# Where a turned activation tile is put together, and when the last one of a unit is joined

## The chip, the cores and the metric

The kernel runs on one core of one Trainium2 chip. The metric is device time in microseconds (us), the median of three runs of the kernel before: 1449.74 us (1449.1 to 1450.11). Engines are named as the profile names them: PE is TensorE, PEld its weight loads, DVE is VectorE, ACT is ScalarE, POOL is GpSimd, SP is the engine whose queue issues most DMAs.

## What is computed

One decoder layer for 256 tokens of width 2048: a mixer (a state-space group and an attention group side by side), and then the squared-ReLU MLP, which the change touches:

```
def squared_relu_mlp(u, w_up, w_down):
    hdn = jax.nn.relu(jnp.einsum('bsd,df->bsf', u, w_up))
    return jnp.einsum('bsf,fd->bsd', hdn * hdn, w_down)

h = h + rmsnorm(ff, norm_mlp_post)      # ff = the MLP of rmsnorm(h, norm_mlp_pre)
```

`w_up` is 2048 x 8192, `w_down` 8192 x 2048, all in float32.

## The kernel before, in words

**Products.** Every float32 operand is split in two parts, `hi` and `lo` (lines 148 and 149: ACT copies `hi`, DVE subtracts it to get `lo`), and a product takes three matmuls: hi by hi, hi by lo, lo by hi. Weights come in blocks of 128 x 2 x 512 by DMA from SP's queue into places called `raw` (four of them, and others that are free for a while, such as `ha` and `uc`), are split into one of five pairs of `hi` and `lo` tiles, and are streamed through PE.

**Units.** A unit (function `unit`) makes two column blocks of 512 for both halves of the tokens (t = 0 and 1), in four PSUM banks `acc`; four further banks `more` take partial sums. It goes through the rows of the weight two blocks of 128 at a time; such a step is called a pair here (index k). Some pairs are done in full (`row_tiles`, lines 368 to 370, 24 matmuls); the others by Strassen's scheme with seven products in place of eight (`seven`, lines 455 to 457, 21 matmuls), which needs sums of weights (tiles `e` and one temporary, line 263) and sums of activations (`sums_of_acts`, lines 414 to 417, made once and kept). After the last seven, `combine_new` (lines 464 to 468) reads the banks `more` and writes four tiles in `room["shared"]`: two in `hb`, two in `wpost`. Its last addition, line 468, reads the last of these banks and writes the fourth tile. After that the unit does its last pair, and the next unit takes over with `acc` and `more` exchanged, so that its first products go to the banks that `combine_new` has read.

**The MLP.** The 8192 hidden columns are made in two halves. Each half has four units of the up projection (in the first half the first of these is made in another way), and then two units of the down projection. I number them up 0 to up 3 and down 0, down 1 in each half; up 0 of the first half is the one made in another way. A unit of the up projection has seven pairs in its order, the sevens at places 1, 3, 4 and 6, and an eighth pair at the end.

**Turned tiles.** At the end of an up unit (`up_end`, line 1491) each of the four shared tiles (two blocks, two halves of tokens) is completed, and a generator `turned` is put into the deque `beside` for it. Its first part (lines 1500 to 1503) applies ReLU and square on ACT, copies the 16-bit halves of the words apart into one of two places (`room["halves"]`, in turn; line 1502), and lets SP issue a DMA transpose that writes back into the shared tile (line 1503). Its second part (lines 1505 to 1508) puts the words together again on ACT (line 1506) into a tile called `junk`, and splits that into the `hi` and `lo` of the activations of the down projection (`sh`, `sl`, or `ah`, `al`). A tile is joined, in the words of the title, when this second part is done.

`unit` starts one first part (`pump_beside`) at each place from 2 on, and does a second part (`land_beside`) when two further places have passed. So the tiles of one up unit are handled within the next unit: the first parts at places 2, 3, 4 and 5, the second parts at 4, 5, 6 and, for the fourth tile, later. After the last seven, `drain_beside` finishes all that is left, ahead of `combine_new`. In an up unit that means that the fourth tile is finished at place 6, too; in a down unit all four have been finished by place 7.

**The order.** Most instructions are ordered by a scheduler under priorities; the splits of weights are issued in a line by `issue_after`. What each engine gets is a fixed queue. Temporaries come from `tmp()`, a ring of four tiles named `r`, used by `sums_of_acts`, `seven` and `combine_new`.

Of the kernel before, what the change touches and what calls it, by code (L numbers as in the profile page):

```python
# [10 lines left out]
F32 = mybir.dt.float32  # L11
# [6 lines left out]
P = 128  # L18
# [21 lines left out]
NB = 512  # L40
# [38 lines left out]
def hymba_layer(ctx: ExitStack, tc: tile.TileContext, x, norm_mix_pre, w_in, conv_w, conv_b, dt_bias, a_log,  # L79
# [34 lines left out]
    def part(k):  # L114
        if k < NK:
            return sh, sl, k
        i, r = divmod(k - NK, NK // 2)
        return (*att[i], r)
# [49 lines left out]
    def tmp():  # L168
        if "own" in room:
            room["own"].rotate(1)  # L170
            return room["own"][0]
        return hp.tile([P, NB], F32, name="r", bufs=4)
# [6 lines left out]
    room = {}  # L179
# [13 lines left out]
    def beside_up(raws, turn, halves=None):  # L193

        room["sums"] = [v[:, k:k + KB] for k in range(0, NK // 2, KB) for v in att[1]]
        b = hp.tile([P, NT, NB], F32, name="hb")
        room["shared"] = [[b[:, t] for t in range(NT)],
                          [hp.tile([P, NB], F32, name="wpost", bufs=2) for _ in range(NT)]]
        a = hp.tile([P, 3 * KB, NB], F32, name="ha")
        in_a = [a[:, k:k + KB] for k in range(0, 3 * KB, KB)]  # L200
        halves = in_a.pop(0) if halves is None else halves
        room["halves"] = deque(halves[:, i].bitcast(U16) for i in range(KB))
        room["raw"], room["turn"], room["acts"], room["chain"] = [*raws, *in_a], turn, act_u, True
        room["of_halves"], room["of_a"] = halves, in_a
        sums_of.clear()

    def beside_down():

        a = hp.tile([P, 3 * KB, 2, S], F32R, name="ha")
        room["sums"] = [a[:, k] for k in range(3 * KB)]  # L210
        room["raw"], room["turn"], room["acts"], room["then"] = [mws[2]], 0, part, more_beside_down
        sums_of.clear()
# [60 lines left out]
    def blocks_of(n):  # L273
        return n if isinstance(n, tuple) else (n * NB, (n + 1) * NB)
# [57 lines left out]
    def drain():  # L332
        while waiting:
            pump()
# [3 lines left out]
    def pump_beside():  # L338

        if not beside:  # L340
            return
        work = beside.popleft()
        with tc.issue_after(newest["act"].ins):
            next(work)
        flying.append([work, 0])

    def land_beside(steps=2):

        for one in flying:
            one[1] += 1  # L350
        if flying and flying[0][1] > steps:
            with tc.issue_after(newest["act"].ins):
                next(flying.popleft()[0], None)
        if not (beside or flying) and "then" in room:
            room.pop("then")()

    def drain_beside():
        while beside or flying:
            pump_beside()
            land_beside(0)  # L360
# [11 lines left out]
    def row_tiles(src, c0, ks, acc, acts, first=True, last=True, lag=0, at_end=None, pumps=1, fetch=fetch, halves=None):  # L372


        held = {}
        n = len(ks)
        for i in range(n + lag):
            if i < n:
                held[i] = weights(src, ks[i] * KB, c0, fetch)
            for t, at in ((0, i), (1, i - lag)):  # L380
                if not 0 <= at < n:
                    continue
                if t and halves and at == n - 1:
                    row_tile(acc[t], t, held[at], ks[at], acts, False, last, slice(0, NB // 2))
                    halves(acc[t])
                    acc[t] = bank()
                    row_tile(acc[t], t, held[at], ks[at], acts, True, last, slice(NB // 2, NB))
                else:
                    row_tile(acc[t], t, held[at], ks[at], acts, first and at == 0, last and at == n - 1)
                if at == n - 1 and at_end:  # L390
                    at_end(t, acc[t])
            pump(pumps)
# [12 lines left out]
    def sums_of_acts(k):  # L405

        if k in sums_of:
            return sums_of[k]
        places = room["sums"][2 * len(sums_of):][:2]
        h_, l_, r = room["acts"](k * KB)  # L410
        with tc.high_priority(offset=AHEAD):
            a, c = (tmp().rearrange("p (i s) -> p i s", s=P) for _ in range(2))
            ah_, al_ = (v[:, r:r + KB].bitcast(F32).rearrange("p j (t s) -> p j t s", t=NT) for v in (h_, l_))
            nc.vector.tensor_tensor(a.rearrange("p (j t) s -> p j t s", t=NT), ah_, al_, op=ALU.add)
            nc.vector.tensor_tensor(c[:, 0:2], a[:, 0::3], a[:, 1:2].to_broadcast([P, 2, P]), op=ALU.subtract)
            nc.vector.tensor_tensor(c[:, 2], a[:, 0], c[:, 1], op=ALU.add)
            nc.vector.tensor_tensor(c[:, 3], a[:, 2], c[:, 2], op=ALU.subtract)
            ch, cl = (v.rearrange("p b (t s) -> p (b t) s", t=NT) for v in places)
            split(ch, cl, c)
        sums_of[k] = ch, cl  # L420
        return ch, cl
# [66 lines left out]
    def unit(src, n, order, last, acc, more, combine, lag=0, at_end=(None, None), first=True, ending=None,  # L488
             ready=None, halves=None):


        cols = blocks_of(n)
        sevens = [k for k, by_seven in order if by_seven]
        for i, (k, by_seven) in enumerate(order):
            if i >= 2:
                pump_beside()
            if i + 1 < len(order) and order[i + 1][1]:
                sums_of_acts(order[i + 1][0])
            if by_seven:
                if k == sevens[0]:  # L500
                    drain()
                    if ready:
                        ready()
                seven(src, *cols, k, acc, more, k == sevens[0], k == sevens[-1])
            else:
                for b in range(2):
                    row_tiles(src, cols[b], [k], acc[b::2], room["acts"], first and i == 0, False,
                              fetch=fetch_next)
            land_beside()
            if k == sevens[-1]:  # L510
                drain_beside()
                combine(more)
        for b in range(2):
            if b and ending:
                ended.append(ending(cols[b], last, acc))
            else:
                row_tiles(src, cols[b], last, acc[b::2], room["acts"], False, True, lag if b else 0, at_end[b],
                          fetch=fetch_last if b else fetch_next, halves=halves if b else None)
# [808 lines left out]
    hp = ctx.enter_context(tc.tile_pool(name="hp", bufs=1, reuse_waits="tile"))  # L1327
# [167 lines left out]
    def turned(t, k, r):  # L1495
        room["halves"].rotate(1)
        halves = room["halves"][0]
        ts = slice(t * P, (t + 1) * P)
        words = r.bitcast(U16)
        nc.scalar.activation(r, r, AF.Relu, scale=rmlp[:, t:t + 1])  # L1500
        nc.scalar.activation(r, r, AF.Square)
        nc.scalar.activation(halves.rearrange("p (h n) -> p h n", h=2), words.rearrange("p (n h) -> p h n", h=2), AF.Copy)
        nc.sync.dma_start_transpose(words.rearrange("p (n s) -> p n s", s=P), halves)
        yield
        whole = hp.tile([P, NB], F32, name="junk")
        nc.scalar.activation(whole.bitcast(U16).rearrange("p (n h) -> p h n", h=2), words.rearrange("p (h n) -> p h n", h=2), AF.Copy)  # L1506
        d_h, d_l, i = part(k)
        split(d_h[:, i:i + 4, ts], d_l[:, i:i + 4, ts], whole.rearrange("p (f s) -> p f s", f=4))
# [17 lines left out]
    for hf in range(2):  # L1526
        if hf:
            beside_up([], 0)
        for fb in range(0 if hf else 2, 8, 2):
            unit(w_ups[hf], fb, orders[("up", hf), fb], (7,), acc, more,  # L1530
                 lambda x: combine_new(room["shared"], x), 0, (up_end(fb, 0), up_end(fb + 1, 1)))
            acc, more = more, acc
        if hf == 0:
            beside_down()
            unit(w_down, 0, orders[("down", 0), 0], (14, 15), acc, more,
                 lambda x: combine_new(in_mw(0), x), 0, (onto(0), onto(1)))
            room["raw"], room["turn"] = [new_mw(2)], 0
            room["sums"] += room["sums"][:4]
            unit(w_down, 2, orders[("down", 0), 2], (12, 14, 15), more, acc,
                 onto_new_mw, 0, (onto(2), onto(3)))  # L1540
# [65 lines left out]
```

## Time and profile before

| | |
|---|---|
| median of three runs | 1449.74 us |
| the profiled execution | 1448.34 us |
| its span, first to last instruction | 1446.6 us |
| busy PE, PEld | 1432.3 us (99%), 1201.5 us (83%) |
| busy DVE, ACT, POOL | 1297.6 us (90%), 1000.4 us (69%), 162.6 us (11%) |
| granted TensorE clock | 0.999 |

A row of the timeline has the start in us from the span's start, the duration in us, engine, line, operation, output and inputs, and in brackets how long the engine had been idle and who ended that. The rows called SPq are the issue of DMAs on SP's queue; what they move lands later. The waits are listed as engine, line, whom it waited for, us in total, number of waits, longest. Matmuls overlap: a row says 0.39 us, but the next starts 0.23 us later. The up units of the second half begin at about 1102, 1144, 1185 and 1227 us, and its down 0 at about 1268 us; down 0 of the first half begins at about 939 us.

### The profile page before, as it was taken

To read this page: it belongs to the slowest core of one execution; us is meant where nothing else is said; L and a number is where in the kernel's file an instruction comes from. 1 tells how busy PE (TensorE), PEld (TensorE's weight loads), DVE (VectorE), ACT (ScalarE), POOL (GpSimd) and SP (SyncE) were. 2 spreads that over 40 slices of the span, in tenths; PEclk is the share of its full clock that TensorE was granted. 3 is DMA by queue.
4 is the path that set the end of the run, shared out by engine and by line. 5 is a ranking of instruction groups with operands and counts; after the bars stand their busy time and mean duration, and the time that the engine had idled before them with its cause. 6 is when DMAs were issued, how large, how long until landed. Compare 5 with 4: busy or idle time off the path is not lost. (4 is left out here: it accounts for less than half of the span.)

```text
span 1446.6 us, 20277 instructions
## 1 busy us (share of the span) xinstructions
PE 1432.3 (99%) x6930; PEld 1201.5 (83%) x6930; DVE 1297.6 (90%) x1881; ACT 1000.4 (69%) x1407; POOL 162.6 (11%) x244
## 2 busy tenths in 40 slices
PE   9999999999999999999999999999999999999998
PEld 8888888888888888888888888878888878877886
DVE  7788888988999778689988999999889989989998
ACT  7577669666666666556667668986565689987664
POOL 0201110131111000011100011011111111111000
PEclk9999999999999999999999999999999999999999
DMA  8977656756888648588976799798888999999864
GB/s 268 273 217 225 190 175 186 236 175 195 232 245 255 192 126 251 168 268 261 275 235 213 203 340 288 197 266 244 257 254 262 253 268 288 247 280 293 264 197 150
DMA packets 201927, 340.31 MB, mean 235 GB/s; under 512 B 45616, under 2 KB 48544, under 8 KB 201824
## 3 DMA queue, kind: packets, MB, share of 16 engines
q1 hardware_dynamic: 174304, 279.72, 62.0%
q0 software_dynamic: 19648, 45.63, 15.5%
q10 hardware_dynamic: 7872, 13.68, 2.8%
q8 instruction: 54, 0.88, 0.3%
q14 instruction: 49, 0.40, 0.1%
HBM read 327.39 MB, written 49.84 MB: 261 GB/s over the span
## 5 line engine op out<-in xcount | busy, mean ns | idle before, releaser
L149 DVE TENSOR_TENSOR lo<-raw,hi 128x1024 fp32r<-128x1024 f32 (+1 forms) x390 | 472.6, 1217 | 82.8 <-ACT hi L148 80.6
L148 ACT ACTIVATE hi<-raw 128x1024 fp32r<-128x1024 f32 (+1 forms) x390 | 406.2, 1048 | 170.2 <-PE acc L370 49.1
L526 PE MATMUL acc<-ua,hi 128*128 128x512 f32 x520 | 141.2, 400 | 0.1
L148 ACT ACTIVATE hi<-e 128x1024 fp32r<-128x1024 f32 x66 | 69.7, 1057 | 53.8 <-DVE e L263 50.2
L526 PEld LDWEIGHTS acc<-ua,hi 128*128 128x128 f32 x520 | 91.2, 189 | 14.2 <-ACT hi L148 0.2
L368 PE MATMUL acc<-hi,ua 128*128 128x512 f32 x228 | 90.4, 396 | 0.4 <-DVE wpost L468 0.4
L368 PE MATMUL acc<-hi,sh 128*128 128x512 f32 x220 | 86.6, 394 | 3.0 <-DVE wpost L468 3.0
L369 PE MATMUL acc<-lo,ua 128*128 128x512 f32 x228 | 89.2, 391 | 0.0
L370 PE MATMUL acc<-hi,ua 128*128 128x512 f32 x228 | 89.1, 391 | 0.0
L149 DVE TENSOR_TENSOR lo<-e,hi 128x1024 fp32r<-128x1024 f32 x66 | 80.4, 1218 | 6.4 <-ACT hi L148 6.2
L370 PE MATMUL acc<-hi,sl 128*128 128x512 f32 x220 | 85.7, 390 | 0.0
L369 PE MATMUL acc<-lo,sh 128*128 128x512 f32 x220 | 85.6, 389 | 0.0
L529 PEld LDWEIGHTS acc<-ua,lo 128*128 128x128 f32 x520 | 76.5, 189 | 8.9
L529 PE MATMUL acc<-ua,lo 128*128 128x256 f32 x520 | 78.8, 281 | 0.0
L456 PE MATMUL acc<-lo,ah 128*128 128x512 f32 x180 | 70.6, 392 | 0.7 <-DVE lo L149 0.7
L457 PE MATMUL acc<-hi,al 128*128 128x512 f32 x180 | 70.1, 389 | 0.0
L455 PE MATMUL acc<-hi,ah 128*128 128x512 f32 x180 | 70.1, 389 | 0.0
L526 PE MATMUL acc<-uc,hi 128*128 128x512 f32 x208 | 61.4, 405 | 0.0
L149 DVE TENSOR_TENSOR lo<-ha,hi 128x1024 fp32r<-128x1024 f32 x48 | 58.3, 1218 | 3.0 <-ACT hi L148 2.7
L148 ACT ACTIVATE hi<-ha 128x1024 fp32r<-128x1024 f32 x48 | 50.2, 1050 | 6.9 <-PE acc L370 2.0
L456 PE MATMUL acc<-lo,ua 128*128 128x512 f32 x137 | 53.4, 390 | 0.2 <-DVE lo L149 0.2
L455 PE MATMUL acc<-hi,ua 128*128 128x512 f32 x137 | 53.5, 391 | 0.0
(565 smaller groups left out, 3717.0 us busy)
## 6 DMA issues: line engine op xcount, KB each, us to landing
raw<-in_w_in_dram SPq DMA_DIRECT2D x154, 512.0 KB, 4.4
raw<-in_w_down_dram SPq DMA_DIRECT2D x70, 512.0 KB, 5.7
raw<-in_w_up_dram SPq DMA_DIRECT2D x65, 512.0 KB, 5.0
raw<-in_w_out_dram SPq DMA_DIRECT2D x38, 512.0 KB, 5.2
raw<-pair SPq DMA_DIRECT2D x59, 256.0 KB, 4.7
pair<-in_w_up_dram POOLq DMA_DIRECT2D x56, 256.0 KB, 5.8
pair<-in_w_down_dram POOLq DMA_DIRECT2D x52, 256.0 KB, 5.9
ha<-in_w_up_dram SPq DMA_DIRECT2D x25, 512.0 KB, 6.8
```

What stands on the lines that cost most here:

```text
L148: return (nc.scalar.activation(hi, src, AF.Copy), nc.vector.tensor_tensor(lo, src, hi.bitcast(F32), op=ALU.subtract))
L149: nc.vector.tensor_tensor(lo, src, hi.bitcast(F32), op=ALU.subtract))
L368: nc.tensor.matmul(dst[:, cs], a_h[:, r, ts], hi[:, j, cs], start=begin and j == 0, stop=False)
L369: nc.tensor.matmul(dst[:, cs], a_h[:, r, ts], lo[:, j, cs], start=False, stop=False)
L370: product[t] = nc.tensor.matmul(dst[:, cs], a_l[:, r, ts], hi[:, j, cs], start=False, stop=end and j == KB - 1)
L455: nc.tensor.matmul(dst, a_h, hi[:, j], start=own and first, stop=False)
L456: nc.tensor.matmul(dst, a_h, lo[:, j], start=False, stop=False)
L457: nc.tensor.matmul(dst, a_l, hi[:, j], start=False, stop=own and last)
L526: nc.tensor.matmul(acc[f], hi[:, j, f * P:(f + 1) * P], u(k0 + j), start=k0 + j == 0, stop=False, skip_group_check=True)
L529: nc.tensor.matmul(acc[f][:, 0], lo[:, j, f * P:(f + 1) * P], u(k0 + j)[:, 0], start=False, stop=k0 + j == NK - 1, skip_group_check=True)
```

## The change

The second part of `turned` takes its tile from `tmp()`, the ring of four, and no longer from the single place `junk`. The fourth shared tile alternates between two places, one `wpost` tile and a tile `junk`: before each up unit `room["last"]` is rotated and its first entry becomes `room["shared"][1][1]`. And `drain_beside` is no longer called after the last seven, so that the fourth tile of an up unit is finished after place 0 of the unit after the next.

```
@@ beside_up
                           [hp.tile([P, NB], F32, name="wpost", bufs=2) for _ in range(NT)]]
+        room["last"] = deque([room["shared"][1].pop(), hp.tile([P, NB], F32, name="junk")])
+        room["shared"][1].append(room["last"][0])
@@ unit
             if k == sevens[-1]:
-                drain_beside()
                 combine(more)
@@ turned
-        whole = hp.tile([P, NB], F32, name="junk")
+        whole = tmp()
@@ the loop over the up units
         for fb in range(0 if hf else 2, 8, 2):
+            room["last"].rotate(1)
+            room["shared"][1][1] = room["last"][0]
             unit(w_ups[hf], fb, orders[("up", hf), fb], (7,), acc, more,
```

No instruction is added or removed; the queues are ordered anew. Line numbers after the change are one or two higher: 468 is 470, 1502 is 1503, 1503 is 1504, 1506 is 1507.

DVE, the end of up 1 of the second half (`lo` is a weight's low part, `hb`, `wpost` and `junk` hold the shared tiles, `sl` is the low part of a turned tile). Before:

```order
L465 TENSOR_TENSOR r<-hb,ps 128x512
L466 TENSOR_TENSOR hb<-acc,r 128x512
L467 TENSOR_TENSOR wpost<-acc,r 128x512
L149 TENSOR_TENSOR lo<-raw,hi 128x1024
L1491 TENSOR_TENSOR hb<-acc,hb 128x512 x2
L149 TENSOR_TENSOR lo<-raw,hi 128x1024
L263 TENSOR_TENSOR e<-ha 128x512
L149 TENSOR_TENSOR sl<-junk,sh 128x4x128
L263 TENSOR_TENSOR e<-e,ha 128x512
L149 TENSOR_TENSOR lo<-ha,hi 128x1024
L468 TENSOR_TENSOR wpost<-acc,wpost 128x512
```

The same place after the change:

```order
L467 TENSOR_TENSOR r<-hb,ps 128x512
L149 TENSOR_TENSOR lo<-raw,hi 128x1024
L468 TENSOR_TENSOR hb<-acc,r 128x512
L469 TENSOR_TENSOR wpost<-acc,r 128x512
L1492 TENSOR_TENSOR hb<-acc,hb 128x512
L470 TENSOR_TENSOR wpost<-acc,wpost 128x512
L1492 TENSOR_TENSOR hb<-acc,hb 128x512
L149 TENSOR_TENSOR lo<-raw,hi 128x1024
```

The last addition of `combine_new` stands two `lo`, two `e`, one `sl` and one `hb` addition earlier.

SP, down 0 of the second half, from the loads of the fourth and fifth pair on (`uc`, `ha` and `raw` are places for weights, `pair` a sum of two weight blocks in DRAM; the transposes go to the shared tiles). Before:

```order
L157 DMA raw<-pair_90 128x512
L158 DMA raw<-in_w_down_dram 128x512
L1503 DMA_TRANSPOSE hb<-ha 128x8x128 x2
L162 DMA uc<-in_w_down_dram 128x2x512 x2
L1503 DMA_TRANSPOSE wpost<-ha 128x8x128
L162 DMA ha<-in_w_down_dram 128x2x512
L157 DMA ha<-pair_91 128x512
L158 DMA ha<-in_w_down_dram 128x512
L1503 DMA_TRANSPOSE wpost<-ha 128x8x128
```

After:

```order
L157 DMA raw<-pair_90 128x512
L158 DMA raw<-in_w_down_dram 128x512
L162 DMA uc<-in_w_down_dram 128x2x512 x2
L1504 DMA_TRANSPOSE hb<-ha 128x8x128 x2
L1504 DMA_TRANSPOSE wpost<-ha 128x8x128
L162 DMA ha<-in_w_down_dram 128x2x512
L157 DMA ha<-pair_91 128x512
L158 DMA ha<-in_w_down_dram 128x512
L1504 DMA_TRANSPOSE wpost<-ha 128x8x128
```

The first two transposes now stand behind the two loads into `uc`.

ACT, the same stage (`hi<-e`, `hi<-ha` and `hi<-r` are the splits of a seven's weights; `ha<-wpost` is the copy of the third tile's halves, and the row with 2x512 puts the first tile together). Before:

```order
L1500 ACTIVATE wpost<-wpost,rmlp 128x512
L148 ACTIVATE hi<-ha 128x1024
L1502 ACTIVATE ha<-wpost 128x1024
L1506 ACTIVATE junk<-hb 128x2x512
L148 ACTIVATE hi<-e 128x1024
L148 ACTIVATE hi<-ha 128x1024
L148 ACTIVATE hi<-r 128x512
```

After:

```order
L1501 ACTIVATE wpost<-wpost,rmlp 128x512
L148 ACTIVATE hi<-ha 128x1024
L1502 ACTIVATE wpost<-wpost 128x512
L148 ACTIVATE hi<-e 128x1024
L148 ACTIVATE hi<-ha 128x1024
L1503 ACTIVATE ha<-wpost 128x1024
L1507 ACTIVATE r<-hb 128x2x512
L148 ACTIVATE hi<-r 128x512
L148 ACTIVATE hi<-raw 128x1024 x3
```

The copy of the halves has moved behind two of the seven's three splits, and still stands ahead of the third and of the next three blocks.

More of the change, by code (lines that the diff above doesn't have):

```diff
@@ L198, in beside_up @@
                           [hp.tile([P, NB], F32, name="wpost", bufs=2) for _ in range(NT)]]
+        room["last"] = deque([room["shared"][1].pop(), hp.tile([P, NB], F32, name="junk")])
+        room["shared"][1].append(room["last"][0])
         a = hp.tile([P, 3 * KB, NB], F32, name="ha")
@@ L510, in unit @@
             if k == sevens[-1]:
-                drain_beside()
                 combine(more)
@@ L1504, in turned @@
         yield
-        whole = hp.tile([P, NB], F32, name="junk")
+        whole = tmp()
         nc.scalar.activation(whole.bitcast(U16).rearrange("p (n h) -> p h n", h=2), words.rearrange("p (h n) -> p h n", h=2), AF.Copy)
@@ L1529, in hymba_layer @@
         for fb in range(0 if hf else 2, 8, 2):
+            room["last"].rotate(1)
+            room["shared"][1][1] = room["last"][0]
             unit(w_ups[hf], fb, orders[("up", hf), fb], (7,), acc, more,
```

## Prediction

> **What bounds the kernel now.** I read the page's busy times first, then PE's waits, then the places of these waits in the timeline.
>
> ```profile
> span 1446.6 us, 20277 instructions
> PE 1432.3 (99%) x6930; PEld 1201.5 (83%) x6930; DVE 1297.6 (90%) x1881; ACT 1000.4 (69%) x1407; POOL 162.6 (11%) x244
> ```
>
> PE is busy for 1432.3 of 1446.6 us. Whatever the change does to the other engines, it can win only time in which PE stands still, at most 14.3 us, and only the part that falls in the MLP. The waits of PE and of its weight loads there:
>
> ```profile
> PE acc L368 <- DVE wpost L468: 3.4, 3, 2.0
> PE ps L369 <- DVE lo L149: 1.2, 2, 0.7
> PE acc L456 <- DVE lo L149: 0.9, 2, 0.7
> PEld acc L368 <- DVE wpost L468: 5.5, 5, 2.4
> ```
>
> The largest is the first product of a unit on a bank that line 468 (the last addition of `combine_new`) must read before. Its weight loads show it five times: these are the five takeovers behind an up unit in which turned tiles are handled (up 2 and up 3 of the first half, up 1, 2 and 3 of the second). One of them in the timeline, and the two that cost most:
>
> ```profile
> 1186.64 0.68 DVE L149 TENSOR_TENSOR sl<-junk,sh 128x512 fp32r<-128x512 f32 x1
> 1187.36 1.39 ACT L1506 ACTIVATE junk<-wpost 128x1024 uint16<-128x1024 uint16 x1 [3.35 <-DVE sl L149]
> 1188.95 0.39 PE L370 MATMUL acc<-hi,ua 128*128 128x512 f32 x1
> 1188.99 0.68 DVE L468 TENSOR_TENSOR wpost<-acc,wpost 128x512 f32<-128x512 f32 x1
> 1189.72 0.50 PE L368 MATMUL acc<-hi,ua 128*128 128x512 f32 x1 [0.38 <-DVE wpost L468]
> ```
>
> ```profile
> 943.42 0.50 PE L368 MATMUL acc<-hi,sh 128*128 128x512 f32 x1 [1.05 <-DVE wpost L468]
> ...
> 1275.55 0.50 PE L368 MATMUL acc<-hi,sh 128*128 128x512 f32 x1 [1.99 <-DVE wpost L468]
> ```
>
> This is a chain of two places that are not free. The fourth tile is put together in `junk`, which the third still holds until DVE has split it (1186.64 to 1187.32): ACT stands idle for 3.35 us. And line 468 writes the `wpost` tile that ACT reads for the fourth (1187.36 to 1188.75): it comes at 1188.99, and PE waits for it.
>
> **What goes: the halts at the takeovers.** After the change line 470 writes the other place, and in DVE's queue it stands before the next unit's work. PE then finds its bank free. The gain: PE's own idle time is 3.4 us, that of its weight loads 5.5 us; a halt costs between the two, because a load that comes late costs a part of its lead as well. I take the middle, 4.4 us. The halt at 1275.55 is 1.99 of it, 2.1 with its restart. The other four give 2.3 us, of which I keep 2.0, because DVE has little to spare there: in the rows by stage (columns: length, then busy time of PE, PEld, DVE, ACT, POOL) up 3 of the second half has DVE busy for 41.05 of 42 us.
>
> ```profile
> 1227.00:1269.00 42.00, 41.97 (x184) 34.10 (x184) 41.05 (x50) 37.99 (x45) 4.89 (x7) 1.00 0.93 250
> ```
>
> **What is moved in the up units: the transposes.** In three of them SP's queue now has the first transpose behind two loads that stood behind it before; so in up 3 of the second half:
>
> ```profile
> 1236.19 1.23 SPq L1503 DMA_TRANSPOSE hb<-ha  x1
> 1237.52 1.26 SPq L162 DMA_DIRECT2D ha<-in_w_up_dram  x2
> ```
>
> ```profile
> 1244.16 1.06 ACT L1502 ACTIVATE ha<-wpost 128x1024 uint16<-128x1024 uint16 x1
> ```
>
> ```profile
> DMA to landing us min/median/max: 2.7/6.8/10.3
> ```
>
> The loads wait for their places until 1237.52, the second somewhat longer, so the transpose starts at about 1238.8, 2.6 us later. Over all transposes the landing takes 2.7 to 10.3 us, median 6.8: it would land at 1245.6. The copy of the third tile's halves (line 1502) needs the place that this transpose reads; ACT comes to it at 1244.16, and 1 us later after the change, since one split now precedes it. It waits 0.5 us at the median and up to 4 us (1238.8 + 10.3 against 1245.2), and the splits behind it on ACT with it; DVE works on others meanwhile. For the three units I take 0.5 us in all on PE; bounds 0 and 3.
>
> **What is moved in down 0 of the second half.** This is the place that decides. The rows of SP, ACT, DVE and PE there:
>
> ```profile
> 1285.34 6.87 SPq L1503 DMA_TRANSPOSE hb<-ha  x2
> 1292.31 1.05 SPq L162 DMA_DIRECT2D uc<-in_w_down_dram  x2
> ```
>
> ```profile
> 1293.57 1.06 ACT L1502 ACTIVATE ha<-wpost 128x1024 uint16<-128x1024 uint16 x1 [2.59 <-DMA hb<-ha]
> 1294.54 1.35 ACT L1506 ACTIVATE junk<-hb 128x1024 uint16<-128x1024 uint16 x1
> ...
> 1297.64 0.61 ACT L148 ACTIVATE hi<-r 128x512 fp32r<-128x512 f32 x1
> ...
> 1300.29 1.04 ACT L148 ACTIVATE hi<-raw 128x1024 fp32r<-128x1024 f32 x1
> ```
>
> ```profile
> 1288.29 2.39 DVE L149 TENSOR_TENSOR lo<-uc,hi 128x1024 fp32r<-128x1024 f32 x2 [0.26 <-ACT hi L148]
> ...
> 1296.82 1.23 DVE L149 TENSOR_TENSOR lo<-e,hi 128x1024 fp32r<-128x1024 f32 x1 [2.48 <-ACT hi L148]
> ```
>
> ```profile
> 1302.65 0.50 PE L369 MATMUL ps<-lo,sh 128*128 128x512 f32 x1 [0.51 <-DVE lo L149]
> ```
>
> Before, ACT already waits 2.59 us for the first transpose at the copy of the third tile; DVE waits 2.48 us for ACT; PE is caught at 1302.65. The first transpose is issued at 1285.34 and lets ACT go at 1293.57, 8.2 us later. After the change the two `uc` loads stand ahead of it. Their places are free when DVE has split what lies in them, at 1288.29 + 2.39 = 1290.7, and the second is issued in half of 1.05 us: the transpose goes at 1291.2, 5.9 us later. With the same 8.2 us it lands at 1299.4. ACT waits at the copy until then. Queued behind it are putting the first tile together, the seven's third split, and the splits of the next three blocks: 1.06 + 1.35 + 0.61 = 3.0 us until the first of these starts, at 1302.4 in place of 1300.29. That is 2.1 us later, and so is the `lo` that PE waits for at 1302.65. PE, no longer halted at 1275.55, comes to this point 2 us earlier and waits the longer: the 2.1 us of that halt are not won. **So this stage costs 2.1 us against before, and gives nothing.** Bounds: with a landing of 10.3 us 2.1 more, 4.2; with one of 2.7 us (1293.9) ACT finds it landed: no cost, and the 2.1 us of the halt are won.
>
> [...]
>
> **The sum.** Four takeovers -2.0, transposes in the up units +0.5, down 0 of the second half +2.1: +0.6 us. The profiled execution took 1448.34 us, 1.7 of it around the span, and would take 1448.9; the median of the runs lies 1.4 higher, at 1449.74, so I forecast **1450.3**. A measurement can tell about 0.2% from no change here, 2.9 us: this is no change. Its own range is 1447.3 to 1452.7. Chance 0.44.
>
> **Rivals.**
>
> *Faster: the transposes land early enough.* Then all of the halts are won, 4.4 us, ACT is no longer idle for `junk`, and the up units cost nothing: 1449.74 - 4.4 = 1445.3. For it: the loads of the weights are no longer held up by a transpose, and DMA engines are less crowded where PE is ahead. Against it: the stage's own rows for landing,
>
> ```profile
> hb<-ha SPq DMA_TRANSPOSE x2, 7.6
> wpost<-ha SPq DMA_TRANSPOSE x2, 9.2
> ```
>
> are all long. It needs the first transpose on the chip by about 1295. Chance 0.24.
>
> *Slower: the delay is handed on along SP's queue.* After the fourth transpose of this stage comes a load into the place that it reads, and everything else behind that:
>
> ```profile
> SPq L162 <- DMA wpost<-ha: 8.6, 2, 7.9
> ```
>
> ```profile
> 1300.52 1.66 SPq L1503 DMA_TRANSPOSE wpost<-ha  x1
> ...
> 1310.81 0.39 SPq L162 DMA_DIRECT2D ha<-in_w_down_dram  x1
> ```
>
> The load waited up to 7.9 us for the landing. If the fourth transpose goes 6 us later, as the first does, the load goes at 1316.8 in place of 1310.81, and pairs 10 and 11 have 6 us less of a lead. If that lead is under 4 us, PE halts for 2 more, and with a first landing of 10.3 us 2.1 are added: 0.6 + 2 + 2.1 = 4.7, that is 1454.4. It decides when the load is issued after about 1315. Against it: DVE is behind at this point anyway, so that part of the delay is the same one. Chance 0.26, with all that is slower by over 2.9 us.
>
> *The change doesn't do what it says.* The ring `r` has four places for `sums_of_acts`, sevens, `combine_new` and now the tiles; if these wait for each other, line 470 comes as late as line 468, and the halts stay: -0, +0.5 and the 2.1 of down 0, 1452.3. Between two tiles the order puts at most three other uses, and those before have long been split; I count it within the no-change half, at 0.06.
>
> **How the numbers follow.** The forecast and the last rival make 0.5 for no change, the first rival 0.24, the second 0.26. The range goes from the first rival's 1445.0, rounded, to 1454.5: beyond are landings over 10 us in several units, or gains from ACT's idle time that I don't count.
>
> **What would show it.** Right: no wait of PE for line 470; the copy of the third tile on ACT waiting about 5 us for a transpose at about 1294 to 1299; the waits of PE for `lo` at about 1300 to 1312 larger than 1.2 and 0.9 us. Wrong: if that copy does not wait, the faster rival holds; if PE waits at pairs 10 and 11, with ACT or DVE waiting for a load, the slower; if PE still waits for line 470, the last.

## The result, and the profile after

The changed kernel takes 1470.2 us (median of 4 runs, 1467.12 to 1476.65) against 1449.42 us (4 runs, 1447.28 to 1450.11): 1.0152 times as long, 95% interval 1.0116 to 1.0187. I had forecast 1450.3, no change, with a range to 1454.5. The profiled execution took 1469.98 us. The page's first lines, to be set beside those of before:

```profile
span 1467.9 us, 20236 instructions
PE 1440.4 (98%) x6930; PEld 1205.2 (82%) x6930; DVE 1296.6 (88%) x1881; ACT 998.7 (68%) x1407; POOL 162.3 (11%) x244
```

The same work, 21 us more span; PE is even busy 8 us longer, with as many matmuls. PE's largest waits from 850 us on (engine, line, whom it waited for, us in total, number, longest):

```profile
PE ps L457 <- ACT hi L148: 5.1, 1, 5.1
PE acc L371 <- DVE lo L149: 4.9, 3, 2.3
PE acc L457 <- ACT hi L148: 3.7, 3, 1.8
```

No wait for line 470 is left: the takeovers are free, as forecast. In their place PE waits for splits of weights. To see where, I counted the matmuls in both timelines; the table says how much later than in the kernel before the same number of them had been started, counted from the start of each span (us; the time is that of before). The first turned tile comes at about 863 us, so what a row has at 834 is to be taken off its later columns. Later rows belong to experiments.

| | 834 | 958 | 1163 | 1205 | 1247 | 1290 | 1333 | 1374, and to the end |
|---|---|---|---|---|---|---|---|---|
| changed | 0.3 | 3.5 | 3.5 | 5.5 | 9.1 | 6.6 | 13.9 | 21.4 |
| ring_only | 0.3 | 0.0 | 0.0 | 1.1 | 2.2 | 2.1 | 2.6 | 3.2 |
| places_drained | 0.0 | 5.0 | 5.0 | 6.3 | 6.1 | 7.6 | 11.2 | 11.2 |
| changed_first_ahead | -0.2 | -0.4 | 0.5 | -1.2 | 0.4 | -0.6 | -1.5 | 6.1 |
| drained_first_ahead | 0.4 | -0.4 | 0.1 | -1.9 | -2.2 | -2.4 | -3.3 | 3.9 |
| drained_first_ahead_low_first | 3.1 | 1.6 | 2.1 | 0.1 | -0.2 | -1.0 | -1.9 | -0.3 |
| changed_plain | 0.8 | 1.4 | 1.4 | 3.0 | 7.4 | 6.6 | 14.2 | 25.6 |
| before_a_place_earlier | -0.3 | -2.1 | -2.1 | -4.1 | -4.6 | -0.4 | -3.0 | -3.0 |
| earlier_split_ahead | 0.0 | -1.2 | -1.2 | -3.2 | -3.0 | -4.5 | -0.2 | 0.1 |

The change loses 8.8 us in the up units, wins 2.5 at the takeover of down 0 of the second half, loses 7.3 in the middle of that unit and 7.4 at its end. One of the up units, up 2 of the second half, row by row (start, duration, engine, line):

```profile
1202.93 1.99 ACT L1503 ACTIVATE ha<-hb 128x1024 uint16<-128x1024 uint16 x2
...
1212.35 1.06 ACT L1503 ACTIVATE ha<-wpost 128x1024 uint16<-128x1024 uint16 x1 [2.79 <-DMA hb<-ha]
```

```profile
1204.00 6.51 SPq L1504 DMA_TRANSPOSE hb<-ha  x2
```

```profile
1214.38 1.23 DVE L149 TENSOR_TENSOR lo<-e,hi 128x1024 fp32r<-128x1024 f32 x1 [2.45 <-ACT hi L148]
```

```profile
1214.40 0.51 PE L457 MATMUL acc<-hi,ah 128*128 128x512 f32 x1 [1.16 <-ACT hi L148]
1215.67 0.50 PE L458 MATMUL acc<-lo,ah 128*128 128x512 f32 x1 [0.76 <-DVE lo L149]
```

ACT copies the first two tiles one behind the other into the two places for halves; the third copy must wait until the first transpose, issued at 1204.00, has landed at 1212.3. The splits of a seven stand behind it on ACT, DVE has nothing else to do in the meantime, and PE stops twice. The same in down 0 of the second half, larger:

```profile
1300.27 2.12 SPq L162 DMA_DIRECT2D uc<-in_w_down_dram  x2
1302.44 5.30 SPq L1504 DMA_TRANSPOSE hb<-ha  x2
```

```profile
1299.02 1.22 DVE L149 TENSOR_TENSOR lo<-uc,hi 128x1024 fp32r<-128x1024 f32 x1
...
1300.76 1.22 DVE L149 TENSOR_TENSOR lo<-uc,hi 128x1024 fp32r<-128x1024 f32 x1
...
1314.95 0.69 DVE L149 TENSOR_TENSOR lo<-r,hi 128x512 fp32r<-128x512 f32 x1 [7.63 <-ACT hi L148]
```

```profile
1312.16 1.06 ACT L1503 ACTIVATE ha<-wpost 128x1024 uint16<-128x1024 uint16 x1 [6.74 <-DMA hb<-ha]
```

```profile
1314.97 0.79 PE L457 MATMUL ps<-hi,sh 128*128 128x512 f32 x1 [5.09 <-ACT hi L148]
```

This is the chain of the prediction: the transpose behind the loads into `uc`, the copy behind the transpose, the splits behind the copy. But DVE frees the `uc` places at 1302.0 and not at 1290.7, so the transpose goes at 1302.44, lands 9.7 us later, and PE stands for over 5 us.

Behind this halt PE was slow for a while. The stretches there (length, then busy time of PE, PEld, DVE, ACT, POOL, granted clock, DMA share, GB/s):

```profile
1310.00:1315.00 5.00, 0.03 (x1) 0.03 (x1) 0.05 (x1) 2.84 (x4) 0.81 (x1) 0.73 0.64 89
1315.00:1320.00 5.00, 5.00 (x12) 3.35 (x13) 4.74 (x7) 5.00 (x6) 0.00 (x0) 0.59 1.08 195
1320.00:1325.00 5.00, 5.00 (x23) 3.91 (x22) 5.00 (x10) 4.97 (x7) 0.55 (x1) 1.00 1.05 224
```

With a granted clock of 0.59, 12 matmuls took the 5.00 us of 22 at 0.23 us each. That is 2.3 us here, and 1.6 and 1.9 us more at two other places (from 1216.7 and from 1363.5 us on, both with a granted clock of 0.50); it also makes PE look busier: the row of the matmul at 1316.71 has 0.63 us, that of the one at 1319.31 0.39.

The end of the same unit. DVE, then PE; lines 1140 to 1147 take up the partial sums, and `al` is the low part of a turned tile:

```profile
1357.26 0.69 DVE L1141 TENSOR_TENSOR mw<-r,mw 128x512 f32<-128x512 f32 x1
...
1367.13 0.70 DVE L1147 TENSOR_TENSOR mw<-mw,r 128x512 f32<-128x512 f32 x1
1367.73 1.30 DVE L149 TENSOR_TENSOR al<-r,ah 128x512 fp32r<-128x512 f32 x2
```

```profile
1363.80 1.22 PE L371 MATMUL acc<-lo,ah 128*128 128x512 f32 x2 [1.92 <-DVE lo L149]
1367.28 0.79 PE L371 MATMUL acc<-lo,sh 128*128 128x512 f32 x1 [2.25 <-DVE lo L149]
```

In the kernel before the last low part of a turned tile was made 28 us ahead of that work:

```profile
1316.59 0.68 DVE L149 TENSOR_TENSOR al<-junk,ah 128x512 fp32r<-128x512 f32 x1
```

So there are two suspects: transposes that come too late (theory A), and, found later, low parts that come too late (theory G). The rivals: the carried tile and the shared ring load ACT and DVE too much (C); first parts of `turned` that stand ahead cost ACT time (D); PE's new order (E); DVE being late as a whole (F); and, at first, that only the carried tile costs (B).

### The profile page after: what moved, and what is told of

It reads as the page before. It is cut to its first block, busy times and chain, and to the rows that moved or that the text cites. A ratio compares the mean times of both kernels' runs of the same rounds, so it can differ in the third digit from the quotient of the medians.

```text
span 1467.9 us, 20236 instructions
## 1 busy us (share of the span) xinstructions
PE 1440.4 (98%) x6930; PEld 1205.2 (82%) x6930; DVE 1296.6 (88%) x1881; ACT 998.7 (68%) x1407; POOL 162.3 (11%) x244
## 5 line engine op out<-in xcount | busy, mean ns | idle before, releaser
L527 PEld LDWEIGHTS acc<-ua,hi 128*128 128x128 f32 x520 | 91.3, 189 | 14.2
L371 PE MATMUL acc<-lo,ua 128*128 128x512 f32 x228 | 89.3, 392 | 0.1
L149 DVE TENSOR_TENSOR lo<-r,hi 128x512 fp32r<-128x512 f32 x66 | 45.4, 688 | 9.3 <-ACT hi L148 9.3
```

Source lines behind the costliest of these rows:

```text
L149: nc.vector.tensor_tensor(lo, src, hi.bitcast(F32), op=ALU.subtract))
L371: nc.tensor.matmul(dst[:, cs], a_h[:, r, ts], lo[:, j, cs], start=False, stop=False)
L527: nc.tensor.matmul(acc[f], hi[:, j, f * P:(f + 1) * P], u(k0 + j), start=k0 + j == 0, stop=False, skip_group_check=True)
```

## The experiments

Each ratio is against the kernel before on the same chip, with its 95% interval.

**The parts of the change.** `ring_only` is the kernel before with `whole = tmp()`. `places_drained` is the changed kernel with

```
             if k == sevens[-1]:
+                drain_beside()
                 combine(more)
```

and `drained_before_down` has `if n == 6: drain_beside()` at that place.

> The kernel before with one part of the change: the turned tile is put together in a temporary of the ring; the fourth shared tile keeps its one place and is finished ahead of combine_new as before. Theory A (the ring lets ACT copy the halves of the first two tiles one behind the other, so that both transposes stand together in SP's queue behind loads that wait for their places, and the third tile's copy waits for their landing): the halts of the up units come with this part alone, 5 to 8 us, and the takeovers still wait: 1453 to 1457 us. Theory B (the loss comes from the fourth tile that is carried into the next unit): no new halt, the 3.4 us that ACT stood idle for the single place are gone: 1446 to 1449 us.

> The changed kernel with all turned tiles finished ahead of combine_new again: the ring and the alternating place are kept, the late joining is undone. Theory A: the takeovers no longer halt PE (4 us won), the up units still lose 5 to 8 us: 1450 to 1453 us, and nothing is lost in down 0. Theory B: the whole loss goes and the takeovers' gain stays: about 1445 us.

> The changed kernel, but in the last up unit of each half the turned tiles are finished ahead of combine_new, so that down 0 starts with no tile of up 2 left over; up 1 and up 2 hand their fourth tile on as in the change. Both theories put the 8.2 us that were lost by 1246 us into the up units and leave them. Theory A: down 0 loses as much as in the changed kernel if its first transposes stand behind the two loads into uc, and nothing where two of them stand ahead: here they do, so about 1456 us. Theory B: down 0 loses nothing as nothing is carried into it: 1456 us too, but with the up units' loss gone as soon as nothing is carried at all. The two part in the other kernels; if this one stays near 1470 us, the order of the transposes is not what costs in down 0.

Measured: 1453.89 us, 1.0043 (1.0028 to 1.0057); 1458.6 us, 1.0074 (1.0056 to 1.0092); 1467.43 us, 1.0138 (1.0125 to 1.0151). Theory B falls: the ring alone makes the kernel slower, and with it the first two transposes already stand together in three of the five up units. The ring alone also frees the takeovers, against my expectation: no wait for line 468 is left in `ring_only`, one of 0.8 us for line 467, and new are two of 0.8 us for low parts of weights, at 890 and 1181 us. The alternating place adds to the loss with the same order on SP's queue: ACT's longest wait at the third copy of an up unit was 3.8 us in `places_drained`. A's figure of 1450 to 1453 was too low, and why the place adds 4.7 us to the ring is not settled. The third kernel missed as well. Both theories had 1456; near 1470, I had written, the order of the transposes would not be what costs in down 0. The trace says otherwise: nothing was gained there because the drained tile's own transpose went behind loads, and ACT stood in line for it:

```profile
ACT r L1509 <- DMA junk<-ha: 16.3, 1, 16.3
```

```profile
1299.91 0.79 PE L370 MATMUL acc<-hi,sh 128*128 128x512 f32 x1 [7.41 <-ACT hi L148]
```

**The transposes on another queue.** `turned_by_act_queue`: `nc.scalar.dma_start_transpose` for `nc.sync.dma_start_transpose` in the changed kernel.

> The changed kernel with the DMA transposes issued from ACT's queue and not from SP's, so that none of them stands behind a load that waits for its place. If the late issue makes the halts (a transpose that waits in SP's queue up to 11 us behind the copy), PE's waits for ACT at about 920, 1214 and 1315 us go, and the time falls by most of 20 us, to 1447 to 1453 us with what the issue costs ACT. If the transfer itself is slow (8 to 10 us from issue to landing), or ACT's and DVE's other work is late, it stays above 1463 us.

Measured: 1486.89 us, 1.0272 (1.0251 to 1.0293), on the side that spoke against A. But it is no test of A, since the issue holds up the splits on the queue where it now stands:

```profile
1309.44 1.38 ACTq L1504 DMA_TRANSPOSE hb<-ha  x1
...
1310.95 6.92 ACTq L1504 DMA_TRANSPOSE hb<-ha  x1
```

**The transposes earlier.** The first part of `turned` under the priority of the loads, in the changed kernel, in the kernel before, and in `places_drained`:

```
-        with tc.issue_after(newest["act"].ins):
+        with tc.issue_after(newest["act"].ins), tc.high_priority(offset=AHEAD):
             next(work)
```

and, in `changed_a_place_earlier`, `if i >= 1: pump_beside()` in place of `if i >= 2`.

> The changed kernel, with the first part of turned (ReLU, square, copy of the halves, transpose) under the same priority as the loads and the splits. In SP's queue the first transpose of down 0 then stands 17 rows earlier, before the loads of the fourth pair into uc, and the second between them; the up units' transposes stand apart, too. Theory A (a transpose that stands late in SP's queue keeps ACT at the copy of the third tile or at the joining of the first, and with it the splits): the long halt of PE at 1315 us and most of those at 920, 1214 and 1361 us go: 1445 to 1453 us. Theory C (the tile that is carried over and the shared ring load ACT and DVE too much at the start of a unit, wherever the transposes stand): above 1463 us.

> The kernel before with the first part of turned under the priority of the loads and splits, nothing else. Theory A: its transposes already stand early enough for all but 2.6 us of ACT's time, and its halts are those of the takeovers, which stay: 1445 to 1450 us, no change or a gain of 1 to 3 us. Theory D (the first part's four ACT instructions, 2.4 us a tile, then stand ahead of splits that PE is waiting for): slower, 1453 us or more; if so, what the changed kernel gains by the same edit has this price in it.

> Ring and alternating place kept, all turned tiles finished ahead of combine_new, and the first part of turned under the priority of the loads. Theory A: the 11 us that ring and places cost go, and the takeovers' gain of 2 to 4 us shows: 1443 to 1448 us. Theory C: what the ring costs stays: 1453 to 1459 us.

> The changed kernel with the first parts started one place (pair) earlier in each unit, from place 1 on. In down 0 of the second half the first transpose then stands ahead of the loads into uc, and the second to fourth still behind them. Theory A: the first halt there shrinks, since the third tile's copy waits for the first transpose alone, and the up units' halts shrink by about half: 1452 to 1460 us. Theory C: more work of the carried tiles falls into the first places of a unit: 1470 us or more.

Measured: 1455.33 us, 1.0044 (1.0031 to 1.0058); 1454.78 us, 1.0040 (1.0026 to 1.0054); 1455.72 us, 1.0043 (1.0029 to 1.0057); 1450.75 us, 1.0013 (1.0003 to 1.0024). Theory A holds in the main: with the first parts of `turned` earlier (the transposes, and ACT's work ahead of them) and nothing else edited, the changed kernel gets back some 15 of its 21 us (1.0152 becomes 1.0044), and C's figure for it is far off. A's sizes were not right: the first lies above A's range, the third in the range that I had given for C, the fourth below A's. ACT's waits at the copies into `ha`, changed and `changed_first_ahead`:

```profile
ACT ha L1503 <- DMA hb<-ha: 13.8, 4, 6.7
```

```profile
ACT ha L1503 <- DMA hb<-ha: 3.5, 2, 2.1
```

From 834 to 1333 us `changed_first_ahead` and `drained_first_ahead` win 1.3 and 3.7 us against the kernel before (table): this is what the change was worth at the takeovers, less what the same edit costs elsewhere. Then both lose over 7 us, so that the third's figure does not speak for C. The kernel before gets slower by the same edit, but elsewhere, in down 0 of the first half, where PE waited 3.1 us at 1010 us for a sum of activations; so D's figure came out, and not at D's place. The last of the four has, against my expectation, no carried tile: begun a place earlier, the fourth tile is joined by place 6. It differs from `places_drained` by when the first parts and their transposes go, and its ratio is 1.0013 where that one's is 1.0074.

**The 7 us at the end.** In `changed_plain` every matmul of the second half's down units is held behind the one before it in the program; `drained_ahead_plain` does so in `drained_first_ahead`.

```
+            if room.get("plain") and pe:
+                order.enter_context(tc.issue_after(pe[0].ins))
+            pe[:] = [nc.tensor.matmul(*given, **flags)]
```

> The changed kernel with PE's matmuls of the second half's down units held in the order of the program. What SP gets is the same row for row; on ACT and DVE under a dozen rows move. In the changed kernel's own order, at the end of down 0, products of the last three blocks and of the next unit's first stand among those of the block before. Theory E (this order makes PE wait for low parts of later blocks while products of earlier ones are ready): the 7.2 us that are lost between 1351 and 1372 us shrink to 2 or less, the 5 us halt at 1315 us stays: 1463 to 1466 us. Theory F (DVE is late by then, and PE waits for it in any order): 1468 to 1471 us.

> The kernel with ring and alternating place, tiles finished ahead of combine_new, first parts under the priority of the loads (1455.7 us), with PE's matmuls of the second half's down units in the order of the program; SP's order is the same row for row. By 1333 us it was 4.2 us ahead of the kernel before and lost 7.1 after that. Theory E: it keeps most of its lead: 1446 to 1449 us. Theory F: 1453 to 1456 us.

Measured: 1469.07 us, 1.0142 (1.0123 to 1.0160), and 1457.44 us, 1.0056 (1.0041 to 1.0071). Theory E falls; F's figure came out for the first and was missed by 1.4 us for the second. The new order had filled a wait with other products, and with it gone the wait itself shows, in `changed_plain`:

```profile
1368.52 0.79 PE L370 MATMUL ps<-hi,al 128*128 128x512 f32 x1 [8.24 <-DVE al L149]
```

PE waits for the low part of the last turned tile, an operand of the unit's last pair. From this came theory G, and

```
+    def after_al(x):
+        with tc.issue_after(room["al"].ins):
+            combine_onto(0, x)
```

where `room["al"]` is the last low part that `turned` makes.

> The changed kernel with PE in program order in the down units (1469.1 us, where PE waited 8.2 us for the low part al of the last turned tile), and in addition that low part ahead of the adds by which DVE takes up the partial sums of down 0 (lines 1140 to 1147). ACT's, SP's and PE's orders are the same row for row. Theory G (the ring no longer makes DVE split each tile before the next; the low parts float down its queue, behind work that comes first by priority, until PE stands at the last pair): the 8 to 11 us lost after 1333 us go, 1459 to 1462 us, and the 6 us halt at 1315 us stays. Theory F (DVE is late as a whole): 1466 us or more.

> Ring and alternating place, tiles finished ahead of combine_new, first parts under the priority of the loads (1455.7 us), with the low part of the last turned tile ahead of the adds that take up the partial sums of down 0; SP's order is the same row for row. By 1333 us that kernel was 4 us ahead of the one before. Theory G: it keeps 3 to 4 of them: 1445 to 1449 us. Theory F: 1453 to 1456 us.

> The changed kernel with first parts a place earlier (1450.8 us), and the low part of the last turned tile ahead of those adds; SP's order is the same row for row. It lost 1.6 us after 1333 us, where its low part stood behind the adds, too. Theory G: 1448 to 1450 us. Theory F: 1450.8 us or a little more.

Measured: 1467.45 us, 1.0114 (1.0092 to 1.0136); 1451.15 us, 1.0005 (0.9992 to 1.0018); 1448.89 us, 1.0000 (0.9986 to 1.0014). The second is the clear one: 1.0043 has become 1.0005 with the low part moved from behind line 1148 to ahead of line 1141. That is between G's range and F's, nearer G's: some 5.5 us are back, and not 7. The first has F's figure, the third G's, but the third's interval overlaps that of `changed_a_place_earlier`. DVE in `drained_first_ahead` and in `drained_first_ahead_low_first`:

```profile
1340.76 0.69 DVE L1141 TENSOR_TENSOR r<-r,acc 128x512 f32<-128x512 f32 x1
...
1349.50 0.69 DVE L1148 TENSOR_TENSOR mw<-mw,r 128x512 f32<-128x512 f32 x1
1350.10 1.29 DVE L149 TENSOR_TENSOR al<-r,ah 128x512 fp32r<-128x512 f32 x2
```

```profile
1346.64 1.28 DVE L149 TENSOR_TENSOR al<-r,ah 128x512 fp32r<-128x512 f32 x2
1347.84 0.67 DVE L1141 TENSOR_TENSOR r<-r,acc 128x512 f32<-128x512 f32 x1
```

The second loses 1.6 us after 1333 in place of 7.1. In `changed_plain_low_first` only part came back (5.6 us are lost there in place of 11.4), because the low part still stood behind five splits of weights and PE still waited 3.7 us for it; its interval overlaps that of `changed_plain`, so the trace speaks for G there and the time alone does not. F falls by the second run.

One thing is mixed in these three: the edit also puts the adds behind splits of weights that stood among them. Other traces part the two. In `places_drained`, `ring_only` and `earlier_split_ahead` (below) the adds stand among the splits as before, the last low part is made ahead of them, at 1346.8, 1340.2 and 1307.6 us, and from 1333 us on these kernels lose 0.0, 0.6 and 0.2 us. With the last low part behind all adds but the last one or behind all, 0.6 us (`before_first_ahead`) and 1.6 us (`changed_a_place_earlier`) were lost, and with the last two so late 7.1 to 7.6 us (`changed`, `changed_first_ahead`, `drained_first_ahead`).

**What remains of the change with both causes out.** `earlier_joined_later_plain` is `changed_a_place_earlier` with `land_beside(steps=3)` and PE in program order. `earlier_split_ahead` is `changed_a_place_earlier` with the tiles' splits under `tc.high_priority(offset=AHEAD)`. `before_a_place_earlier` is the kernel before with `if i >= 1: pump_beside()`.

> The changed kernel with first parts started a place earlier, second parts one place later after them (so that the fourth tile is carried over again), and PE's matmuls of the second half's down units in the order of the program. If late transposes and PE's order are all that the change lost by, ACT waits for no transpose, no takeover holds PE, and what the change was to win shows: 1443 to 1447 us. If the carried tile itself costs (more of ACT and DVE at the start of a unit), 1452 us or more.

> The changed kernel with first parts a place earlier and the splits of all turned tiles under the priority of the weights' splits, so that none of their low parts floats down. The kernel before with the first parts a place earlier took 1445.7 us, and 4.4 of it were one halt at the takeover of down 0, for line 468. If late transposes and late low parts are what the change lost by, this kernel has neither, and no such halt: 1441 to 1446 us. If the alternating place and the ring cost something of their own: 1448 to 1452 us.

> The kernel before with the first parts started one place earlier, nothing else. Theory A (what costs is ACT waiting in line for a transpose that stands late): the two waits of 2.6 us at the third tile's copy go, the fourth tile is joined earlier and line 468 holds PE less: 1445 to 1448 us, at best 4 us won. If the gain of the earlier start belongs to the changed kernel alone, it stays at 1449 us.

Measured: 1454.1 us, 1.0023 (1.0007 to 1.0039), 1444.78 to 1456.65 over 12 runs; 1450.08 us, 1.0001 (0.9991 to 1.0010); 1445.67 us, 0.9976 (0.9966 to 0.9985). The last beats both kernels, without any part of the change. The first has the figure that I had given for a cost of the carried tile, the second that for a cost of ring and place; the second should have beaten the last, and does not. In its down 0 the first transpose now goes at 1269.14 us, but the second still stands behind the loads into `uc`, and the fourth tile's copy waits for it; SP and ACT there:

```profile
1288.76 2.12 SPq L162 DMA_DIRECT2D uc<-in_w_down_dram  x2
1290.92 1.49 SPq L1504 DMA_TRANSPOSE hb<-ha  x1
```

```profile
1297.34 1.06 ACT L1503 ACTIVATE ha<-wpost 128x1024 uint16<-128x1024 uint16 x1 [3.44 <-DMA hb<-ha]
```

In `before_a_place_earlier` both transposes go ahead of them, and ACT does not wait (the copy shown is the third tile's):

```profile
1284.38 3.33 SPq L1503 DMA_TRANSPOSE hb<-ha  x2
1289.13 1.56 SPq L162 DMA_DIRECT2D uc<-in_w_down_dram  x2
```

```profile
1290.29 1.04 ACT L1502 ACTIVATE ha<-wpost 128x1024 uint16<-128x1024 uint16 x1
```

So theory A goes on working there, and the expectation, which took late transposes to be out, was wrong: the kernel had won 4.6 us from 834 to 1290 us and lost 4.4 of them by 1333 (table). In the profile of the first the copies into `ha` and `mw` waited for 7.4 and 4.2 us in all, and PE stood 4.4 us at 1310. That the carried tile, the ring or the place cost something of their own besides is not excluded by these figures. The kernel that won keeps one large halt, for line 468 at the takeover of down 0:

```profile
1272.94 0.80 PE L368 MATMUL acc<-hi,sh 128*128 128x512 f32 x1 [4.22 <-DVE wpost L468]
```

**Two tries at that halt.** `before_two_places_earlier` calls `pump_beside()` at every place; `before_earlier_joined_earlier` is `before_a_place_earlier` with `land_beside(steps=1)`.

> The kernel before with the first parts of turned started from place 0 on, two places earlier, nothing else. The fourth tile is then joined by place 5, and line 468 finds its tile free at every takeover. If that joining is what holds line 468, no halt for it is left: 1441 to 1445 us. If the first tiles come too early (ACT at the start of a unit, or the last additions of the unit before), or if the order in down 0, where the transposes stand between the loads into uc, holds ACT: 1447 us or more.

> The kernel before with the first parts a place earlier (1445.7 us) and the second parts one place later than those and not two. The fourth tile is joined by place 5. If ACT does not wait for a landing for it: 1441 to 1445 us. If a landing takes longer than the one place in between (6 us; ACT stood 2.6 us at the third copy in the kernel before), ACT waits at the joinings, and it is slower than 1447 us.

Measured: 1453.33 us, 1.0029 (1.0018 to 1.0040), and 1453.98 us, 1.0032 (1.0017 to 1.0047). No halt for line 468 is left in either, and both are slower: ACT now waits for landings. In the second it is again a second transpose of down 0 that went behind the loads into `uc`, at 1301.01 us:

```profile
ACT junk L1506 <- DMA hb<-ha: 7.3, 1, 7.3
```

The profiled executions of these two took 1457.66 and 1461.88 us, 4.3 and 7.9 above the medians, so their waits can be larger than usual.

## Why the prediction was wrong, step by step

**The takeovers, -2.0 kept of 4.4:** right in mechanism. No wait for line 470 is left, and in `drained_first_ahead`, where least else disturbs, PE won 3.7 us from 834 to 1333. But the ring alone did it: `ring_only` has no such wait either. The halt at 1275.55, which I gave up, was won at first: 2.5 us between 1247 and 1290.

**The transposes in the up units, +0.5:** this step failed. From 834 to 1247 us the change lost 8.8 us, and with the takeovers that it won there about 10. I priced one copy's wait for a landing at the median of all landings, and let DVE "work on others meanwhile". But the first two transposes go together, the third copy waits for a landing of over 8 us, and DVE had no others: it stood 2.45 us for ACT in the rows above. The bound of 3 took the same cover for granted. With the first parts earlier the loss from 834 to 1247 us is 0.6 us (`changed_first_ahead`).

**Down 0 of the second half, +2.1 (0 to 4.2):** right in mechanism, mis-sized, and just beyond its bound. ACT waited 6.74 us where I said 5; PE stood 5.25 us from one start to the next. From 1247 to 1333 us the stage cost 4.8 us against before. I took the time at which the `uc` places come free, 1290.7, from the trace of before. In the changed kernel it was 1302.0: of these 11.3 us the units before explain up to 9.1 (table, 1247); where the rest arose was not traced.

**The end of down 0:** missing from the sum, 7.4 us; a second step that failed. The order already showed the last two `al` rows behind line 1147. I read DVE's order only at the takeover. `junk`, a single place, forces each low part to be made before the next tile can be joined, all but the last one: in `before_first_ahead` that one came at 1358.0 us, with `junk`. The ring of four lets more of them slip, but it need not: in `ring_only` and `places_drained` all were made ahead of the adds. Why two came last in the changed kernel, by priority or by the late transposes, is argued and not shown.

**The slow clock behind halts:** missing too, some 5 to 6 us (the 2.3, 1.6 and 1.9 us of the three places above), spread over the steps above.

**The signs that I had named:** PE has no wait for line 470, and the third copy on ACT waits, later and longer than I said. Of the waits of PE for `lo` there was one of 1.7 us at 1300.30, before that copy waited at all; the large wait was for `hi`. The signs were those of the mechanism and said nothing of its size.

**The rivals:** "handed on along SP's queue" came nearest. Its number, 1454.4, was far too low, and pairs 10 and 11 were not the place; that it lay on the right side is no merit of its mechanism.

Shown by experiments: the late first parts with their transposes (some 15 us) and the late low parts (5.5 us of the 7 that are lost at the end), against a gain of about 1 to 4 that the change does make. Only argued: why a longer ring makes the scheduler put the transposes and the last low parts later. Open: why the alternating place costs 4.7 us more than the ring alone.

## What to carry to other kernels

A single buffer can be worth its wait: it forces the work on what it holds to be done before the next comes. Before giving it more places, look in the new order at where every instruction that it used to force has gone, up to the last use of its result. And a wait that stands in line on an engine is priced by what stands behind it: check that the engine that would work meanwhile has anything to do.

## What the runs showed of the hardware

In the changed kernel the granted clock fell in or behind some halts of PE and not with others. A halt is counted here as the time by which a matmul starts later than 0.23 us behind the one before. Between 100 and 1430 us the trace of the changed kernel has 0.50 from 1216.69 us for 3.41 us, from 1312.26 for 6.83 and from 1363.46 for 6.83, and 1.00 everywhere else; that of the kernel before has 1.00 all through, also behind its halt at 1275.55, 2.14 us so counted. In the changed kernel, halts of 1.99 and 1.03 us at 920 us cost nothing more: the clock stayed at 1.00. Halts of 1.32 and 1.03 us at 1214 us, shorter in sum, had 0.50 behind them, and the 8 matmuls there cost 1.6 us more than at the usual 0.23 us (the columns are those of the stretches above):

```profile
916.32:919.73 3.41, 2.16 (x10) 1.47 (x8) 0.85 (x2) 1.47 (x2) 0.81 (x1) 1.00 1.25 249
919.73:923.15 3.42, 2.07 (x8) 1.50 (x9) 2.85 (x3) 3.42 (x5) 0.00 (x0) 1.00 1.25 263
```

```profile
1213.28:1216.69 3.41, 1.53 (x5) 1.04 (x6) 2.31 (x3) 3.41 (x6) 0.55 (x1) 1.00 0.95 280
1216.69:1220.10 3.41, 3.41 (x9) 2.64 (x8) 3.41 (x5) 3.41 (x5) 0.00 (x0) 0.50 1.18 268
```

In the stretch from 1216.69 us matmuls started 0.43 us apart. What decides with which halt the clock falls was not shown.

Of two transposes issued one right behind the other, the second mostly took longer to issue here. In the traces of the kernel before and of the changed one there are six such pairs on SP's queue, with less than 0.4 us from the end of one issue to the start of the next. The second took 3.07 to 4.92 us, the first 1.24 to 3.48, and in five of the six the second was the longer; the other 44 transposes took 1.23 to 4.17 us, 1.25 at the median. On ACT's queue, in `turned_by_act_queue`, a pair took 1.38 and 6.92 us (above). What the second one waits for these runs don't tell.
